# The seven-product input projection of an FFN, worked on two tiles at a time

## The chip, the cores and the metric

The kernel runs on one core of a Trainium2 chip. The metric is the device time of one execution in microseconds (us). The engines named here are TensorE (PE in the profile, with PEld for its weight loads), VectorE (DVE), ScalarE (ACT), GpSimd (POOL) and SyncE (SP), which issues the DMAs. SBUF is the on-chip memory of 128 partitions, PSUM the accumulators into which TensorE writes, in banks of 128 x 512 f32.

## The reference

Two layers of a decoder trunk on a residual stream h of 512 positions x 1024 channels, in f32. The FFN is computed four times, twice in each layer, with 2816 hidden columns:

```
def swiglu(h, w_in, w_out):
    gate, up = jnp.split(h @ w_in, 2, axis=-1)
    return (jax.nn.silu(gate) * up) @ w_out

h <- LN(alpha*h + 0.5*SwiGLU_a(h))            # FFN before mixing
h <- LN(alpha*h + W_o [GDN | SB | MLA](h))    # mixer
h <- LN(alpha*h + 0.5*SwiGLU_b(h))            # FFN after mixing
h <- h + sigmoid(h W_g) * (p[i] W_p)          # per-layer input embedding
```

The change concerns `h @ w_in`, the silu and the product of gate and up: the in-projection.

## The kernel before

An f32 operand is split into two fp32r parts, a high part `hi` (a cast) and a rest `lo = x - hi`, and each product is three matmuls, hi·hi, hi·lo and lo·hi, into one accumulator. The 2816 hidden columns are 22 tiles of 128. A tile has a gate and an up half, each 128 columns x 1024 rows of w_in, and a result of 128 x 512 for each half. In each FFN the first `NC` = 2 tiles are computed so. The other 20 go by a scheme of seven block products (Strassen in Winograd's form): the quarters of a tile's weights are a11, a12 (the gate half against the first and the second 512 channels) and a21, a22 (the same of the up half); sums of them, s1 to s4, and sums of quarters of the activations, t1 to t4, are multiplied, and the results are added up. A product is 4 steps of k x 3 matmuls of 256 columns, so a tile costs 7 x 12 = 84 matmuls, an in-projection 1680.

What a tile needs around them:

- Weights. `Weights` (lines 48 to 118) prepares blocks of 1024 columns, three blocks ahead of the one in use, in a pool of 4 hi and 4 lo buffers. For the seven products, `add_sums` (lines 78 to 107) puts two quarters of 512 in a block: four loads of a pair's tiles by eight DMAs of 256 KB, four sums of 512 columns a tile (line 96, VectorE), a cast for each of the seven items (line 97, ScalarE), and a subtraction for each (line 99): on VectorE for s1, s2 and s3, on GpSimd for a11, a12, a22 and s4.
- Accumulators. `open_tile` (line 510) takes one bank from each of two pools, psI for gate and psA for up. Each pool has two banks, so two tiles can be in flight; the banks of pools psB and psC are not used here.
- Evictions. `product` copies the results of b11, t1 and t2 to SBUF slabs on ScalarE (lines 503, 505 and 507). `close_tile` (lines 512 to 519) adds the gate half to a slab (514), applies silu on ScalarE, adds and copies the up half in three operations of 256 columns (516 to 518), and multiplies (519), on VectorE.

A tile framework schedules the program: it decides from a model of its own in which order each engine gets its instructions, and it adds the waits. The source order is therefore not the order on an engine; the order is fixed at build time, and each engine runs its list in order.

Behind the in-projection the out-projection multiplies the g tiles with w_out: `split_g` (lines 541 to 549) splits units of two g tiles into `gs` buffers, or, for four of the eleven units, into `old`, the buffers of the activations' hi and lo parts, which come free only after the last product that reads them. Its matmuls have 512 columns (`mm3`).

Of the kernel before, what the change touches and what calls it, by code (L numbers as in the profile page):

```python
# [17 lines left out]
P = 128  # L18
# [9 lines left out]
LAST = 4  # L28
OPT = [
# [18 lines left out]
class Weights:  # L48
# [29 lines left out]
    def add_sums(self, fs, sums, first=False):  # L78

        nc = self.nc  # L80
        rest = ("s1", "s4", "s2", "a22", "s3")
        if first:
            todo = [(0, "a11"), (0, "a12"), (1, "a11"), (1, "a12")] + [(f, n) for f in range(2) for n in rest]
        else:
            todo = [(f, n) for f in range(2) for n in ("a22", "a11", "a12", "s1", "s2", "s4", "s3")]
        quarters = [None, None]

        def one(f, name, hi, lo):
            if quarters[f] is None:
                r0, r1 = self.load(fs[f][0], sums("raw")), self.load(fs[f][1], sums("raw"))  # L90
                quarters[f] = {"a11": r0[:, 0:512], "a21": r0[:, 512:1024], "a12": r1[:, 0:512], "a22": r1[:, 512:1024]}
            q = quarters[f]
            if "s1" not in q and (name == "s1" or not first):
                for s, x, y, op in (("s1", "a21", "a22", ALU.add), ("s3", "a11", "a21", ALU.subtract), ("s2", "s1", "a11", ALU.subtract), ("s4", "a12", "s2", ALU.subtract)):
                    q[s] = sums(s)
# [3 lines left out]
            e.tensor_tensor(out=lo, in0=q[name], in1=hi.bitcast(F32), op=ALU.subtract)  # L99

        for i in range(7):
            def make(i=i):
                hi, lo = self.pair()
                for j in range(2):
                    one(*todo[2 * i + j], hi[:, j * 512:(j + 1) * 512], lo[:, j * 512:(j + 1) * 512])
                return hi, lo
            self.blocks.append(make)
# [12 lines left out]
def trunk(  # L120
# [128 lines left out]
    def new_xT():  # L249
        xT["hi"] = xp.tile([P, KD, S], F32R, tag="xh", name=nm("xh"))  # L250
        xT["lo"] = xp.tile([P, KD, S], F32R, tag="xl", name=nm("xl"))
# [76 lines left out]
    def plan_ffn(l, w_in, w_out):  # L328
# [4 lines left out]
        def sums(name):  # L333
            if ln_s["new"]:
                ln_s["new"] = False
                ln_s["n"] = 0
                u = unit("su").rearrange("p a b -> p (a b)")
                ln_s["r"] = 0
                ur = unit("wr").rearrange("p a b -> p (a b)")
                ln_s["w"] = [None, None, None, ur[:, 0:1024], ur[:, 1024:]]  # L340
                ln_s["s"] = [lnp.tile([P, 1024], F32, tag="lng", name=nm("sa")), lnp.tile([P, 1024], F32, tag="lnb", name=nm("sb")), u[:, 0:1024], u[:, 1024:]]
            if name == "raw":
                ln_s["r"] += 1
                return ln_s["w"][(ln_s["r"] - 1) % 5]
            i = ln_s["n"] = ln_s["n"] + 1
            i = (i - 1) % 8
            return ln_s["s"][i // 2][:, (i % 2) * 512:(i % 2 + 1) * 512]
# [4 lines left out]
        for f in range(NC, NF, 2):  # L352
            W.add_sums([tile_in(f), tile_in(f + 1)], sums, f == NC)
# [52 lines left out]

    ple_s = {}
# [12 lines left out]
    def ffn(l, ln_i):  # L420
# [3 lines left out]
        def part(ps, us, c0, c1):  # L424
            for j in range(2):
                for k in range(KD):
                    hi, lo = (u.rearrange("p (j k c) -> p j k c", k=4, j=2)[:, j, k % 4, :] for u in us[k // 4])
                    mm3(ps[j][:, c0:c1], hi, lo, xT["hi"][:, k, c0:c1], xT["lo"][:, k, c0:c1], k == 0, k == KD - 1)

        def g_(f):  # L430
            if f % 4 == 0:
                GA.append(unit("g"))
            return GA[f // 4][:, f % 4, :]

        def evac(f, ps):
            s = slab("s")
            act(s, ps[0], AF.Silu)
            V.tensor_tensor(out=g_(f), in0=s, in1=ps[1], op=ALU.mult)
# [3 lines left out]
        for f in range(2):  # L442
            part(pss[f], us[f], 0, 256)


        XH, XL = xT["hi"], xT["lo"]
        full = [unit("xf"), unit("xf")]

# [6 lines left out]
        R = {"b11": (XH[:, 0:4, 0:256], XL[:, 0:4, 0:256]), "b21": (XH[:, 4:8, 0:256], XL[:, 4:8, 0:256]), "b22": (XH[:, 4:8, 256:512], XL[:, 4:8, 256:512])}  # L455
        todo = []
        for name, x, y in (("t1", B[1, 2], B[1, 1]), ("t3", B[2, 2], B[1, 2]), ("t2", B[2, 2], "t1"), ("t4", B[2, 1], "t2")):
            if name == "t3":
                hl = [XH[:, 0:4, 256:512], XL[:, 0:4, 256:512]]
            else:  # L460
                hl = unit(name, F32R).rearrange("p a b -> p (a b)").rearrange("p (w k c) -> p w k c", w=2, k=4)
                hl = [hl[:, 0], hl[:, 1]]
# [6 lines left out]
        def split_t(name, hl, d):  # L469
            A.copy(hl[0], d)  # L470
            G.tensor_tensor(out=hl[1], in0=d, in1=hl[0].bitcast(F32), op=ALU.subtract)
# [5 lines left out]
        for f in range(2):  # L477
            part(pss[f], us[f], 256, 512)
            evac(f, pss[f])
        for f in range(2, NC):  # L480
            u = (W.next(), W.next())
            ps = banks(f % 2 == 1)
            part(ps, u, 0, 512)
            evac(f, ps)
        if NC > 2:
            split_t(*todo[1])
        blk = {"n": 0}

        def product(ps, name, start):
# [784 lines left out]
```

## Time and profile before

| | |
|---|---|
| median of 3 runs | 2470.91 us (2469.47 to 2471.38) |
| profiled execution | 2470.22 us |
| its span | 2468.4 us, 1.8 us less |
| TensorE busy | 2290.9 us, 93% of the span |
| VectorE busy | 1685.1 us, 68% |
| GpSimd busy | 1216.6 us, 49% |
| ScalarE busy | 1022.8 us, 41% |
| mean granted TensorE clock | 0.970 of full speed |

The four in-projections lie at 41.4 to 283.3, 814.3 to 1057.9, 1269.4 to 1507.9 and 2041.0 to 2284.7 us, from the first seven-product matmul to the last; these are 967.7 us of the span. The record of a matmul is longer than the distance to the next one, because matmuls overlap in the pipeline: the distance between two starts tells the rate. The same holds, less so, for the other engines.

### The profile page before, as it was taken

How to read it: one execution, taken by the hardware profiler on the slowest of the kernel's cores; microseconds unless marked ns; L12 is line 12 of the kernel's file. 1: busy time of each engine (PE TensorE's matmuls, PEld its weight loads, DVE VectorE, ACT ScalarE, POOL GpSimd, SP SyncE). 2: the span in 40 equal slices, each digit the busy share in tenths (PEclk: the TensorE clock that was granted, in tenths of full speed). 3: DMA queues.
4: the chain of work that ended last, by engine and by line, in shares of the span. 5: the costliest groups of instructions: out<-in, count | busy, mean ns of one | idle time of the engine just before them, and what ended most of it. 6: DMA issues, size and time to landing. Idle time of an engine off the chain costs nothing. (4 is left out here: it accounts for less than half of the span.)

```text
span 2468.4 us, 39369 instructions
## 1 busy us (share of the span) xinstructions
PE 2290.9 (93%) x15554; PEld 2000.7 (81%) x15554; DVE 1685.1 (68%) x2449; ACT 1022.8 (41%) x1929; POOL 1216.6 (49%) x785
## 2 busy tenths in 40 slices
PE   7999999998898899999989999999979997999998
PEld 7899888765777899988788998887657777999877
DVE  8899706559565899842589995075694668998334
ACT  4454513652452444532244544146424424445222
POOL 5555643434345655554365555424343466555542
PEclk9999999998999899999999999999999998999999
DMA  4333333211012233332323333332110122333322
GB/s 134 102 89 96 112 93 84 70 42 56 24 48 69 73 89 96 99 115 71 100 73 91 94 110 99 93 88 61 35 56 27 44 69 76 95 91 103 115 85 69
DMA packets 271272, 199.81 MB, mean 81 GB/s; under 512 B 12688, under 2 KB 236016, under 8 KB 271088
## 3 DMA queue, kind: packets, MB, share of 16 engines
q1 hardware_dynamic: 271088, 197.30, 27.2%
q8 instruction: 122, 2.00, 0.3%
q14 instruction: 62, 0.51, 0.1%
HBM read 195.17 MB, written 2.10 MB: 80 GB/s over the span
## 5 line engine op out<-in xcount | busy, mean ns | idle before, releaser
L74 POOL TENSOR_TENSOR wlo<-wraw,whi 128x1024 fp32r<-128x1024 f32 (+3 forms) x209 | 443.1, 2134 | 413.8 <-ACT whi L72 373.8
L72 ACT CAST whi<-wraw 128x1024 fp32r<-128x1024 f32 (+3 forms) x194 | 200.5, 1035 | 394.4 <-PE pi L405 156.7
L99 POOL TENSOR_TENSOR wlo<-wraw,whi 128x512 fp32r<-128x512 f32 x144 | 230.1, 1614 | 168.0 <-ACT whi L97 109.2
L499 PE MATMUL pa<-t,whi 128*128 128x256 f32 x640 | 191.3, 299 | 51.6 <-DVE g L518 27.9
L99 POOL TENSOR_TENSOR wlo<-wr,whi 128x512 fp32r<-128x512 f32 x96 | 153.9, 1616 | 132.7 <-ACT whi L97 127.9
L501 PE MATMUL pa<-t,wlo 128*128 128x256 f32 x640 | 177.8, 287 | 11.1 <-DVE wlo L99 11.1
L499 PE MATMUL pi<-xh,whi 128*128 128x256 f32 x640 | 185.5, 290 | 1.4 <-ACT whi L97 1.4
L501 PE MATMUL pa<-xh,wlo 128*128 128x256 f32 x640 | 182.1, 285 | 3.3 <-POOL wlo L99 3.3
L501 PE MATMUL pi<-xh,wlo 128*128 128x256 f32 x640 | 183.1, 286 | 0.0
L500 PE MATMUL pi<-xl,whi 128*128 128x256 f32 x640 | 183.0, 286 | 0.0
L500 PE MATMUL pa<-t,whi 128*128 128x256 f32 x640 | 182.9, 286 | 0.0
L499 PE MATMUL pa<-xh,whi 128*128 128x256 f32 x640 | 181.6, 284 | 0.0
L500 PE MATMUL pa<-xl,whi 128*128 128x256 f32 x640 | 181.6, 284 | 0.0
L499 PEld LDWEIGHTS pa<-t,whi 128*128 128x128 f32 x640 | 124.1, 194 | 67.2 <-DVE g L518 26.2
L187 ACT ACTIVATE s<-s 128x512 f32<-128x512 f32 x80 | 50.6, 632 | 258.2 <-DVE s L514 258.0
L97 ACT CAST whi<-su 128x512 fp32r<-128x512 f32 x160 | 91.7, 619 | 136.4 <-PE pi L500 118.9
L519 DVE TENSOR_TENSOR g<-g,s 128x512 f32<-128x512 f32 x80 | 140.2, 1752 | 1.1
L99 DVE TENSOR_TENSOR wlo<-su,whi 128x512 fp32r<-128x512 f32 x120 | 127.9, 1089 | 5.8 <-ACT whi L97 5.8
L501 PEld LDWEIGHTS pa<-t,wlo 128*128 128x128 f32 x640 | 121.9, 194 | 11.9 <-DVE wlo L99 11.9
L499 PEld LDWEIGHTS pi<-xh,whi 128*128 128x128 f32 x640 | 125.1, 195 | 3.8 <-ACT whi L97 1.9
L501 PEld LDWEIGHTS pa<-xh,wlo 128*128 128x128 f32 x640 | 123.5, 193 | 3.9 <-POOL wlo L99 3.9
L501 PEld LDWEIGHTS pi<-xh,wlo 128*128 128x128 f32 x640 | 124.9, 195 | 0.5 <-POOL wlo L99 0.4
(492 smaller groups left out, 7319.1 us busy)
## 6 DMA issues: line engine op xcount, KB each, us to landing
wraw<-in_ffa_w_in_dram SPq DMA_DIRECT2D x112, 256.0 KB, 3.8
wraw<-in_ffb_w_in_dram SPq DMA_DIRECT2D x112, 256.0 KB, 3.5
wraw<-in_ffa_w_out_dram SPq DMA_DIRECT2D x44, 512.0 KB, 3.8
wraw<-in_ffb_w_out_dram SPq DMA_DIRECT2D x44, 512.0 KB, 3.8
wraw<-in_mix_w_in_dram SPq DMA_DIRECT2D x40, 512.0 KB, 3.9
wr<-in_ffa_w_in_dram SPq DMA_DIRECT2D x64, 256.0 KB, 3.0
wr<-in_ffb_w_in_dram SPq DMA_DIRECT2D x64, 256.0 KB, 3.0
wraw<-in_mix_w_o_dram SPq DMA_DIRECT2D x16, 512.0 KB, 3.8
```

What stands on the lines that cost most here:

```text
L72: self.nc.scalar.copy(hi[:, :width], raw[:, :width])
L74: (eng or self.nc.gpsimd).tensor_tensor(out=lo[:, c], in0=raw[:, c], in1=hi[:, c].bitcast(F32), op=ALU.subtract)
L97: nc.scalar.copy(hi, q[name])
L99: e.tensor_tensor(out=lo, in0=q[name], in1=hi.bitcast(F32), op=ALU.subtract)
L187: i = A.activation(*a, **k)
L499: T.matmul(dst, ah, bh, start=start and k == 0, stop=False, skip_group_check=True)
L500: T.matmul(dst, ah, bl, start=False, stop=False, skip_group_check=True)
L501: T.matmul(dst, al, bh, start=False, stop=k == 3, skip_group_check=True)
L519: V.tensor_tensor(out=g, in0=g, in1=s, op=ALU.mult)
```

## The change

Two neighbouring tiles (a pair) are worked on together. `add_quads` replaces `add_sums`: a block is one quarter item of both tiles, 1024 columns wide. Per pair there are four DMAs of 512 KB instead of eight of 256 KB, four sums instead of eight, seven casts and seven subtractions instead of fourteen each. s3 and s4 are written over a21 and a12. Only the subtractions of a22 and a12 are GpSimd's (`LOG`), the other five are VectorE's. Seven raw slots of 1024 columns take the place of five.

Each product runs over both tiles before the next one starts. `open_pair` takes the four banks of psI and psA for every second pair, and the four of psB and psC for the others, so four tiles are in flight, and four slabs per pair out of the same pool of four. t3 also is copied out by ScalarE (line 496 of the changed kernel), into the slab that holds t1's copy; `close_pair` then needs one addition of 512 columns for the up half (507) in place of three operations of 256. The order of the products is t4 b11 b21 t1 t2 b22 t3, in the first pair b11 b21 t1 t2 t4 b22 t3. Besides, the activations' hi and lo buffers become one tile, and the out-projection takes its first four accumulators from psI and psA alone (`ps0`).

```
+LOG = ("a22", "a12")
-    def add_sums(self, fs, sums, first=False):
+    def add_quads(self, parts, slot, eng, first=False):
+        nc, q = self.nc, {}
+        def one(name):
+            if not q:
+                for n in ("a22", "a11", "a12", "a21"):
+                    q[n] = self.load([(lambda r: r.rearrange("p (k c) -> p k c", k=4), parts[n])], slot("raw"))
+                q["s3"], q["s4"] = q["a21"], q["a12"]
+            if "s1" not in q and name[0] == "s":
+                q["s1"], q["s2"] = slot("s1"), slot("s2")
+            for s, x, y, op in (("s1", "a21", "a22", ALU.add), ("s2", "s1", "a11", ALU.subtract), ("s4", "a12", "s2", ALU.subtract), ("s3", "a11", "a21", ALU.subtract)):
+                if s == name:
                     nc.vector.tensor_tensor(out=q[s], in0=q[x], in1=q[y], op=op)
+            hi, lo = self.pair()
             nc.scalar.copy(hi, q[name])
-            e = nc.vector if name in ("s1", "s2", "s3") else nc.gpsimd
+            eng(name).tensor_tensor(out=lo, in0=q[name], in1=hi.bitcast(F32), op=ALU.subtract)
+        def product(ps, name, w):
+            for f in range(2):
+                bank_ = ps["up" if up else "gate"][f]
...
+                elif name == "t3":
+                    A.copy(ps["x"][f][:, 0:256], dst)
-        def open_tile():
-            return {"gate": ibank(), "up": bank(), "s": slab("s"), "s5": slab("s5", 256)}
+        def open_pair(i):
+            b = banks4() if i % 2 == 0 else banks() + banks(True)
+            return {"gate": b[:2], "up": b[2:], "s": [slab("s"), slab("s")], "x": [slab("x"), slab("x")], "begun": set()}
-            V.tensor_tensor(out=g[:, 256:], in0=s5, in1=up[:, 256:], op=ALU.add)
-            V.tensor_copy(s5, up[:, 256:])
-            V.tensor_tensor(out=g[:, 0:256], in0=s5, in1=up[:, 0:256], op=ALU.add)
-            V.tensor_tensor(out=g, in0=g, in1=s, op=ALU.mult)
+        def close_pair(f0, ps):
+            g = g_(f0, 2)
+            for f in range(2):
+                V.tensor_tensor(out=ps["s"][f], in0=ps["s"][f], in1=ps["gate"][f], op=ALU.add)
+                act(ps["s"][f], ps["s"][f], AF.Silu)
+                V.tensor_tensor(out=g[:, f], in0=ps["x"][f], in1=ps["up"][f], op=ALU.add)
+            for f in range(2):
+                V.tensor_tensor(out=g[:, f], in0=g[:, f], in1=ps["s"][f], op=ALU.mult)
-        ps0 = banks() + [ibank(), ibank()]
+        ps0 = banks4()
```

VectorE in the middle of the first in-projection, before (s, s_44: slabs; su, sa, sb: sums; pi, pa: banks; wlo: a block's lo part):

```order
L514 TENSOR_TENSOR s_783<-s_783,pi_781 128x512
L99 TENSOR_TENSOR wlo_889<-su_273,whi_888 128x512
L516 TENSOR_TENSOR g_906<-s_44_784,pa_782 128x256
L96 TENSOR_TENSOR su_273<-wraw_1044 128x512
L96 TENSOR_TENSOR su_273<-wraw_1047,su_273 128x512
L517 COPY s_44_784<-pa_782 128x256
L518 TENSOR_TENSOR g_906<-s_44_784,pa_782 128x256
L99 TENSOR_TENSOR wlo_969<-sa_275,whi_968 128x512
L519 TENSOR_TENSOR g_906<-g_906,s_783 128x512
L96 TENSOR_TENSOR sa_275<-wraw_1185,wr_274 128x512
L99 TENSOR_TENSOR wlo_1001<-sb_276,whi_1000 128x512
```

The same stretch of VectorE in the changed kernel (x: the new slabs; wq, wraw: raw slots; s_70, s_80: the sums s1 and s2):

```order
L505 TENSOR_TENSOR s_983<-s_983,pi_979 128x512
L507 TENSOR_TENSOR g_969<-x_984,pa_980 128x512
L509 TENSOR_TENSOR g_969<-g_969,s_982 128x512
L92 TENSOR_TENSOR wq_270<-wq_270,s_70_1219 128x1024
L95 TENSOR_TENSOR wlo_1222<-s_69_1218,whi_1221 128x1024
L507 TENSOR_TENSOR g_969<-x_985,pa_981 128x512
L92 TENSOR_TENSOR s_80_1451<-wraw_1344,wq_270 128x1024
L95 TENSOR_TENSOR wlo_1251<-s_70_1219,whi_1250 128x1024
L509 TENSOR_TENSOR g_969<-g_969,s_983 128x512
L92 TENSOR_TENSOR wraw_1344<-wraw_1341,wraw_1344 128x1024
L95 TENSOR_TENSOR wlo_1282<-wq_270,whi_1281 128x1024
L92 TENSOR_TENSOR s_81_1452<-s_80_1451,wraw_1341 128x1024
```

A tile's chain of 512- and 256-column operations has become one of 512- and 1024-column operations for two tiles, with the next pair's sums and subtractions between them, and the subtractions of a11 and s4 now stand on VectorE.

ScalarE at the end of the first in-projection, before (gs and old: the split of g for the out-projection; nea: a preparation for the mixer):

```order
L505 COPY s_117_2954<-pi_2951 128x256
L546 CAST gs_3183<-g_906 128x1024
L546 CAST gs_3216<-g_1415 128x1024
L546 CAST gs_3379<-g_2435 128x1024
L72 CAST whi_3032<-wraw_3030 128x1024
L507 COPY s_2953<-pa_2952 128x256
L187 ACTIVATE s_2953<-s_2953 128x512
L195 ACT_TABLE_LOAD
L187 ACTIVATE nea_3933<-par_3902 128x8
L72 CAST whi_3080<-wraw_3078 128x1024
L546 CAST old_3250<-g_1925 128x1024
L546 CAST old_3249<-g_1415 128x1024
```

The same place in the changed kernel:

```order
L187 ACT_TABLE_LOAD
L179 ACTIVATE nea_3701<-par_3670 128x8
L496 COPY x_2609<-pc_2605 128x256
L73 CAST whi_2850<-wraw_2848 128x1024
L496 COPY x_2610<-pc_2606 128x256
L528 CAST old_3019<-g_1434 128x1024
L528 CAST old_3019<-g_1898 128x1024 x2
L528 CAST old_3019<-g_2362 128x1024
L528 CAST gs_2854<-g_462 128x1024
L528 CAST gs_2887<-g_462 128x1024
```

Before, six casts into gs stand ahead of the last tile's copies; now the copies of the last product and the four casts into old stand ahead of the first cast into gs. On TensorE all matmuls of the out-projection now stand behind the last product; before, some stood between the products of the last tiles. This holds for the first and the third in-projection; in the second and fourth the casts into gs stand first.

## Rows read from the trace of the kernel before

**Rows 1.** the page's first part: the span, and each engine's busy time.

```profile
span 2468.4 us, 39369 instructions
PE 2290.9 (93%) x15554; PEld 2000.7 (81%) x15554; DVE 1685.1 (68%) x2449; ACT 1022.8 (41%) x1929; POOL 1216.6 (49%) x785
```

**Rows 2.** windows of the four in-projections: length, busy us (x instructions) by engine, clock, DMA.

```profile
41.40:283.30 241.90, 221.89 (x1721) 214.63 (x1720) 214.02 (x239) 116.24 (x232) 136.77 (x84) 0.98 0.32 91
...
sum 967.70, PE 885.10 PEld 856.43 DVE 860.72 ACT 458.64 POOL 552.25; mean PE 221.27 PEld 214.11 DVE 215.18 ACT 114.66 POOL 138.06
```

**Rows 3.** windows of 180 us in the middle of each in-projection, same columns.

```profile
80.00:260.00 180.00, 167.86 (x1352) 163.61 (x1353) 163.78 (x195) 86.05 (x181) 102.37 (x66) 1.00 0.35 100
...
sum 720.00, PE 675.67 PEld 659.20 DVE 659.48 ACT 343.13 POOL 405.27; mean PE 168.92 PEld 164.80 DVE 164.87 ACT 85.78 POOL 101.32
```

**Rows 4.** timeline, TensorE, steady: start, duration, engine, line, operation, tiles.

```profile
152.06 0.28 PE L499 MATMUL pa<-xh,whi 128*128 128x256 f32 x1
152.18 0.28 PE L500 MATMUL pa<-xl,whi 128*128 128x256 f32 x1
...
272.66 0.39 PE L403 MATMUL pb<-whi,gs 128*128 128x512 f32 x1
272.89 0.39 PE L404 MATMUL pb<-wlo,gs 128*128 128x512 f32 x1
```

**Rows 5.** waits of TensorE in 80 to 260 us: total, times, longest.

```profile
PE pa L499 <- DVE g L518: 6.4, 9, 1.2
PE pa L499 <- ACT s L503: 5.3, 6, 1.0
```

**Rows 6.** windows of the first microseconds of two in-projections, columns as in rows 2.

```profile
41.40:60.00 18.60, 12.65 (x80) 12.04 (x78) 18.44 (x14) 8.44 (x17) 15.54 (x8) 0.82 0.16 43
814.30:835.00 20.70, 11.77 (x78) 10.87 (x77) 20.67 (x15) 8.38 (x15) 17.75 (x9) 0.76 0.13 38
```

**Rows 7.** waits of TensorE in 814.3 to 855 us, as rows 5.

```profile
PE pa L501 <- DVE wlo L99: 5.1, 1, 5.1
PE pi L501 <- DVE wlo L99: 3.9, 2, 3.3
```

**Rows 8.** timeline, VectorE, before the second in-projection, little on GpSimd beside it.

```profile
800.26 0.68 DVE L96 TENSOR_TENSOR sa<-wraw,wraw 128x512 f32<-128x512 f32 x1
800.86 0.68 DVE L96 TENSOR_TENSOR sa<-wraw 128x512 f32<-128x512 f32 x1
...
806.42 1.22 DVE L453 TENSOR_TENSOR xf<-xh,xl 128x1024 f32<-128x1024 f32 x1
807.55 2.32 DVE L465 TENSOR_TENSOR xf<-xf,xf 128x1024 f32<-128x1024 f32 x1
```

**Rows 9.** operations on the FFN tiles: engine, operation, tiles, count, duration min/median/max ns, starts, shape.

```profile
L518 DVE TENSOR_TENSOR g<-s,pa x80: 407/420/422, 70.6 to 2285.9; 128x256 f32<-128x256 f32 x80
L519 DVE TENSOR_TENSOR g<-g,s x80: 679/1779/2583, 72.7 to 2286.4; 128x512 f32<-128x512 f32 x80
L547 DVE TENSOR_TENSOR gs<-g,gs x28: 1210/1214/3428, 270.1 to 2297.9; 128x1024 fp32r<-128x1024 f32 x28
L547 DVE TENSOR_TENSOR old<-g,old x16: 1212/2311/3434, 287.5 to 2294.5; 128x1024 fp32r<-128x1024 f32 x16
```

**Rows 10.** GpSimd by line and shape: busy us, mean ns, idle before.

```profile
L74 POOL TENSOR_TENSOR wlo<-wraw,whi 128x1024 fp32r<-128x1024 f32 x139 | 353.7, 2552 | 318.1 <-ACT whi L72 285.2 <-issue 26.0 <-DVE gs L547 6.8
L99 POOL TENSOR_TENSOR wlo<-wraw,whi 128x512 fp32r<-128x512 f32 x144 | 230.1, 1614 | 168.0 <-ACT whi L97 109.2 <-PE pi L501 53.2 <-PE pa L501 4.2
```

**Rows 11.** timeline, ScalarE, end of the first in-projection.

```profile
267.08 2.94 ACT L546 CAST gs<-g 128x1024 fp32r<-128x1024 f32 x3
...
280.68 1.28 ACT L195 ACT_TABLE_LOAD   x1
...
284.38 3.89 ACT L546 CAST old<-g 128x1024 fp32r<-128x1024 f32 x4
```

**Rows 12.** page, DMA issues: count, KB each, us from issue to landing.

```profile
wraw<-in_ffa_w_in_dram SPq DMA_DIRECT2D x112, 256.0 KB, 3.8
```

More of the change, by code (lines that the diff above doesn't have):

```diff
@@ L76, in add @@
         self.blocks.append(make)
-    def add_sums(self, fs, sums, first=False):
[L80 to L95, printed above, removed]
+    def add_quads(self, parts, slot, eng, first=False):
[9 more added lines that the diff above has]
+                if s == name:
@@ L109, in fill @@
+            return hi, lo
+        for name in ("a11", "a12", "s1", "s2", "a22", "s4", "s3") if first else ("a22", "a11", "a12", "s1", "s2", "s4", "s3"):
+            self.blocks.append(lambda name=name: one(name))
     def fill(self, n):
@@ L331, in tile_in, with slot, quarter_rows @@
                       rows(w_in, l, kh * 4, 4, j * D_FF + f * P, j * D_FF + (f + 1) * P)) for j in range(2)] for kh in range(2)]
-        def sums(name):
+        def slot(name):
             if ln_s["new"]:
[L335 to L347, printed above, removed]
+                ln_s["new"], ln_s["r"] = False, 0
+                ln_s["w"] = [x[:, i * 1024:(i + 1) * 1024] for x in (unit("wq").rearrange("p a b -> p (a b)") for _ in range(2)) for i in range(2)]
+            if name != "raw":
+                return lnp.tile([P, 1024], F32, tag="lng" if name == "s1" else "lnb", name=nm(name))
+            ln_s["r"] += 1
+            i = (ln_s["r"] - 1) % 7
+            return ln_s["w"][i // 2] if i % 2 == 0 else None
+        def quarter_rows(f, i, j):
+            return rows(w_in, l, j * 4, 4, i * D_FF + f * P, i * D_FF + (f + 2) * P)
         for f in range(NC):
@@ L352, in plan_ffn @@
         for f in range(NC, NF, 2):
-            W.add_sums([tile_in(f), tile_in(f + 1)], sums, f == NC)
+            W.add_quads({f"a{i + 1}{j + 1}": quarter_rows(f, i, j) for i in range(2) for j in range(2)}, slot,
+                        lambda name: G if name in LOG else V, f == NC)
         for n in range(2):
@@ L422, in ffn, with part @@
         GA = []
[L424 removed]
+        X = xT["x"]
+        XH, XL = xT["hi"], xT["lo"]
+        def part(ps, us, c0):
             for j in range(2):
@@ L477, in ffn @@
         for f in range(2):
[L478 removed]
+            part(pss[f], us[f], 256)
             evac(f, pss[f])
[L480 to L489, printed above, removed]
[L490 to L507 removed]
@@ L539, in ffn @@
+        for i, f in enumerate(range(NC, NF, 2)):
+            ps = open_pair(i)
+            for name in ("b11", "b21", "t1", "t2", "t4", "b22", "t3") if i == 0 else ("t4", "b11", "b21", "t1", "t2", "b22", "t3"):
+                product(ps, name, W.next())
+                if i == 0 and name == "b21":
+                    split_t(*todo[1])
+            close_pair(f, ps)
         NU = NF // 2
@@ L556, in split_unit @@
             if not spare:
-                old = [xp.tile([P, KD, S], F32R, tag=tag, name=nm("old")) for tag in ("xh", "xl")]
-                spare.extend(o[:, 4 * i:4 * i + 4, :] for o in old for i in range(2))
+                old = xp.tile([P, 2, KD, S], F32R, tag="x", name=nm("old"))
+                spare.extend(old[:, j, 4 * i:4 * i + 4, :] for j in range(2) for i in range(2))
             return spare[len(HL) - 5]
```

84 lines of the change are left out of this document (27 added, 57 removed).

## The prediction

> **What bounds the kernel now.** I read the page's engine totals first, then windows over the four in-projections and over their middles, then TensorE's waits in these, then single durations on VectorE and GpSimd, and last ScalarE at an in-projection's end. The reader should see in the totals that TensorE is busy 93% of the span [rows 1], which alone would say that there is little to win. The windows say more. The four in-projections take 967.7 us [rows 2]. Steady seven-product matmuls start 0.12 us apart (152.06, 152.18), those of 512 columns 0.23 us apart [rows 4]. An in-projection window holds 1680 of the first kind and about 41 of the second (1721 in all), which at these distances need 201.6 + 9.4 = 211.0 us; four need 844. So about 124 us are lost in the four windows, to waits and to a low clock, and this is what the change can win. The change leaves the number of matmuls as it is.
>
> Where the loss lies: in the middles, 720 us hold 5443 matmuls (1352 in the first window) [rows 3], worth 653 us; 67 us are lost there, 2.06 us in each pair of 168 matmuls (22.2 us where 20.16 would do). TensorE waits there only for L499, the first product of a tile into a bank, and for the operations that empty that bank: L518 of VectorE, 9 times, and the copy L503 of ScalarE, 6 times [rows 5]. Two tiles hold all banks, so each tile's start waits for an earlier tile's emptying. VectorE is busy 659 of these 720 us, 91.6%: it comes late because it is nearly full, and it is full because its operations stretch. A 512-column operation from SBUF follows the next one 0.60 us later when alone (800.26, 800.86), a 1024-column one after 1.13 [rows 8]; the multiplication L519 of the same 512 columns takes 1779 ns at the median, 679 at the least, while L518, which reads PSUM, stays between 407 and 422 ns [rows 9]. GpSimd's 405 us of the 720 [rows 3] are what stands beside the stretched ones. The rest, 124 - 67 = 57 us, is at starts and ends. The first window of 18.6 us holds 80 matmuls (9.6 us), the second of 20.7 us 78 (9.4 us), at granted clocks of 0.82 and 0.76 [rows 6]; the longest waits there are for lo parts that VectorE makes (5.1 and 3.3 us) [rows 7].
>
> **The change part by part.** *Evictions and sums on VectorE.* Per pair, before: 14 SBUF operations of 512 for sums and lo parts, two additions (L514) and two multiplications of 512, six operations of 256. Alone: 18 x 0.6 + 6 x 0.45 = 13.5 us. Measured, 91.6% of 22.2 = 20.35 us, so 6.85 us of stretch for 56% x 22.2 = 12.5 us of GpSimd, 0.55 us for each. After: four sums and five lo parts of 1024, 9 x 1.13 = 10.2; two multiplications, two additions L505 and two L507 of 512, 6 x 0.6 = 3.6; together 13.8 us alone. The own work hardly changes; what changes is GpSimd's, from eight halves to two lo parts of 1024 per pair, at 2.55 us each [rows 10] 5.1 us. At 0.55 this gives a stretch of 2.8 us and 16.6 us for VectorE, against the 20.16 that TensorE needs. The bounds: no stretch, 13.8; each of the nine wide operations at the 2.31 us of the split into old, the multiplications at 1.78 [rows 9], 9 x 2.31 + 2 x 1.78 + 4 x 0.6 = 26.8 us, which would pass TensorE. I take 16.6, since in this count two operations of GpSimd can only meet a few of VectorE's.
>
> At the multiplication L519, alone 679 ns and with GpSimd busy 1779, against the steady 407 to 422 of L518, the trace shows that only operations with both inputs in SBUF stretch [rows 9]. The Trainium skill ("SBUF — State Buffer", section Who interferes with whom) says that such an operation and a GpSimd operation that reads SBUF exclude one another, for the whole instruction. The trace agrees in kind. By that rule two blocks of 2.55 us would add at most 5.1 us a pair, an estimate, and VectorE would need 18.9 us; that speaks for the change even in its harder form.
>
> *ScalarE.* Seven casts of 1024 (2.94 us for three [rows 11], 0.98 each) 6.9 us, eight copies of 256 at some 0.36 and two silus: about 11 of 20.16 us. It was busy 343 of 720 us [rows 3], 10.6 a pair. Its load costs nothing; its order may, below.
>
> *Banks.* Four tiles in flight instead of two. The pair that starts finds the banks of the pair before last, emptied about 16 us ago by the walk below. The waits of rows 5 go. What comes next is a wait for a lo part, the blocks being three ahead. I walked the new orders with the durations above, beginning at the end of a pair's last product: VectorE has emptied that pair's banks 7 us later; the lo parts of s1, s2, s4 and s3 are ready at 3.4, 6.3, 9.1 and 11.4 us and wanted at 8.6, 11.5, 14.4 and 17.3. Margins of 5 to 6 us, more than the 2.8 (and the 5.1) of stretch. A pair is then bound by TensorE. I count 0.2 us a pair of small losses, 36 pairs, 7 us; before, the same pairs lost 2.06 each, 74.
>
> *DMAs.* The same 2 MB a pair, in four issues of 512 KB instead of eight of 256 KB; each of the old took 3.8 us to land [rows 12]. Seven raw slots let the loads of a pair go out before the one ahead is done. They land before they are wanted by the walk, and cost nothing; if this cover goes, s1 is late by some 1 to 5 us a pair.
>
> *Starts.* The first pair still makes nine wide lo parts and sums on VectorE with no blocks ahead of it. Before, the two windows of rows 6 lost 9.0 and 11.3 us (length less matmuls by 0.12). After, with order b11 b21 t1 t2, the lo part of s2 is the late one, by my walk 2 us in the second in-projection, with a granted clock that falls after the wait; I take 2 + 5 + 1.5 + 1.5 = 10 us for the four first pairs and 3 for the plain tiles ahead of them.
>
> *Ends.* Here the change makes it worse. In the first and third in-projection ScalarE makes the copies of t3, a cast, and then four casts into old (3.89 us [rows 11]) before it casts the first gs for the out-projection. In before six gs casts stood ahead (267.08, beside the last tiles), and matmuls of the out-projection filled TensorE's waits. After, all of them stand behind the last product; the last copy ends 1.9 us after it, the four old casts 5.8, gs 6.9, and its lo part, queued behind four of VectorE, about 9. Only the matmuls that need no lo part can start before. I count 7 us idle plus some 2.5 at a lower clock: from rows 6, 0.82 over 18.6 us is 6.7 us at half speed, each of which costs half. So 9.5 us each at two ends; at the other two, where gs goes first, 1.5 each. Together 22 us. Bounds: 1.5 at each end (6), and 14 at the bad ones (31).
>
> *The rest.* The merged hi and lo tile and the mixer's order, moved in some dozens of places by an instruction or two, I cost at nothing, between -4 and +6 us; 1526 us of the span do not belong to the in-projections.
>
> The sum: 124 us lost before; after 7 + 10 + 3 + 22 = 42. The gain is 82 us, on the profiled execution of 2470.2 us (2468.4 + 1.8): 2388. The median lies 0.7 higher: 2389. Since the walk takes every operation at its ordinary duration I add 2 us: **2391 us**, 3.2% faster. The likeliest case's own range is 2375 to 2410.
>
> **The rivals.**
> *A. A queue ties the pairs together.* All four slabs of the pool belong to one pair. ScalarE copies b11 of the next pair into one of them, which has to wait until VectorE's multiplication of the pair before (L509) has read it; behind the copy wait the casts of the next blocks, and behind these TensorE. For it: ScalarE works strictly in order, and is idle in half of its time, waiting for others; VectorE's lead over it is two or three operations. Against it: the walk has L509 done 1 us ahead of b11's copy when two additions come promptly. If each pair loses 1 us, 36 us come back: 2427; it lies between 2410 and 2445. The same number would come from loads that are late.
> *B. Better than the walk.* The ends cost 1.5 us each and the starts half: 16 + 7 us back, 2366 to 2374. For it: the scheduler's order could hide the old casts behind matmuls that wait for no lo part.
> *C. Nothing to win.* VectorE still needs 21 to 22 us a pair, since a 1024-column operation waits longer for GpSimd, and only starts gain: 2450 to 2470. For it, 807.55 with 2.32 us for a wide one [rows 8].
> *D. Slower.* VectorE becomes the bound. Each of its nine wide operations meets GpSimd and takes 2.31 us; 26.8 us a pair from the bound above, 4.6 more than now, over 36 pairs +166, less some 20 of better starts: about 2615. It decides from the point where VectorE's work on a pair passes 22.2 us. For it: the split into old shows 2311 ns as its median [rows 9], and VectorE has taken over a11's and s4's subtraction. Against it: those splits stand right behind an in-projection, where GpSimd works on the lo parts of w_out one after the other (2.55 us each [rows 10]), while here it is busy 5.1 of 20 us.
>
> **How the numbers follow.** The forecast's case 58%, A 20%, B 13%, C 4%, D 5%. The range from 2366 (B) to 2440 (all but the upper end of A) leaves out D, C and little else. A measurement of this kernel can tell 0.2%, 4.9 us, from no change: the forecast, A and B and the greater part of C are faster, 0.92; 0.02 for the same; D and what I may have overlooked 0.06.
>
> **What would show it.** In the changed profile the middles should have some 1480 to 1500 matmuls in 180 us instead of 1352, with no waits of TensorE on evictions; VectorE at 16 to 17.5 us a pair, 80 to 87%, and GpSimd near 25%; a gap of about 7 us on TensorE behind the last product of the first and third in-projection, on casts and lo parts of gs, and none of that size at the other two. Waits for ScalarE's casts, spread over all pairs, would show A; wide operations of VectorE at over 2 us throughout D. I am wrong if the middles stay at 22 us a pair.

## The result, and the profile after

The changed kernel takes 2403.74 us (median of 4 runs, 2402.83 to 2404.15) against 2471.14: a ratio of 0.972, 95% interval 0.970 to 0.974. The forecast was 2391, between 2366 and 2440. The profiled execution's span is 2402.4 us, 66.0 less than before. The page's first lines, where the span is and which engines lost work:

```profile
span 2402.4 us, 38041 instructions
PE 2278.9 (95%) x15554; PEld 2002.6 (83%) x15554; DVE 1449.0 (60%) x2089; ACT 1033.4 (43%) x1729; POOL 913.5 (38%) x545
```

Against [rows 1] VectorE lost 236 us of busy time and GpSimd 303, TensorE 12. Where the 66 us come from is seen when the span is cut at the same places in both kernels: first seven-product matmul, last matmul of the out-projection, and so on. One of these places needs care. In the changed kernel's fourth FFN two seven-product matmuls start at 1996.82 us, ahead of 44 matmuls of the two plain tiles, which take 5.28 us; everywhere else in the two kernels the plain tiles come first. The cut there is therefore put at 2002.10, so that each window holds the same work as the kernel before's (2231 matmuls from there on in both). Windows of the changed kernel (length, then busy us by engine with the instructions, granted clock, DMA share, GB/s):

```profile
40.25:378.70 338.45, 327.31 (x2219) 304.79 (x2218) 184.25 (x193) 148.32 (x213) 117.81 (x50) 0.98 0.32 96
378.70:814.96 436.26, 399.76 (x2851) 318.42 (x2849) 280.00 (x570) 187.10 (x395) 171.96 (x153) 0.92 0.20 56
814.96:1143.80 328.84, 326.58 (x2231) 304.39 (x2230) 196.21 (x197) 148.86 (x216) 126.71 (x50) 0.99 0.32 98
1143.80:1244.54 100.74, 89.44 (x486) 77.13 (x484) 62.16 (x63) 32.83 (x44) 46.13 (x21) 0.92 0.32 99
1244.54:1577.00 332.46, 325.26 (x2220) 303.09 (x2219) 181.79 (x191) 145.94 (x210) 113.98 (x48) 0.99 0.31 93
1577.00:2002.10 425.10, 393.64 (x2850) 312.74 (x2849) 279.95 (x568) 187.20 (x394) 175.19 (x154) 0.94 0.20 58
2002.10:2332.30 330.20, 326.00 (x2231) 304.18 (x2230) 196.50 (x199) 149.04 (x216) 119.20 (x48) 0.99 0.31 97
2332.30:2402.40 70.10, 59.61 (x261) 48.18 (x259) 34.92 (x43) 16.86 (x23) 23.33 (x11) 0.94 0.25 83
```

The same cuts of the kernel before:

```profile
41.40:395.30 353.90, 333.89 (x2220) 307.38 (x2219) 248.24 (x281) 145.84 (x263) 191.30 (x108) 0.99 0.31 91
395.30:814.30 419.00, 385.68 (x2851) 306.11 (x2849) 274.22 (x569) 186.63 (x396) 178.23 (x155) 0.96 0.20 57
814.30:1171.20 356.90, 335.20 (x2231) 308.90 (x2230) 254.28 (x288) 146.95 (x264) 193.26 (x108) 0.98 0.31 92
1171.20:1269.40 98.20, 88.80 (x485) 76.39 (x484) 63.90 (x65) 32.90 (x47) 48.17 (x21) 0.95 0.29 86
1269.40:1619.90 350.50, 332.61 (x2220) 305.50 (x2220) 246.24 (x279) 143.08 (x257) 190.24 (x108) 0.99 0.32 93
1619.90:2041.00 421.10, 387.83 (x2849) 308.67 (x2848) 274.37 (x570) 188.12 (x398) 177.18 (x156) 0.96 0.20 57
2041.00:2398.10 357.10, 334.09 (x2231) 307.90 (x2230) 254.40 (x287) 145.22 (x263) 193.92 (x107) 0.98 0.31 92
2398.10:2468.40 70.30, 59.53 (x261) 48.02 (x259) 34.93 (x43) 16.81 (x23) 23.26 (x11) 0.94 0.24 83
```

The four FFNs (first, third, fifth, seventh row) fall from 1418.4 to 1330.0 us, 88.4 less. The rest of the program gives back a quarter of that. The first layer's mixer (second row) rises from 419.0 to 436.3 us, at a granted clock of 0.92 instead of 0.96, and the second layer's (sixth row) from 421.1 to 425.1, at 0.94 instead of 0.96. The stretch between the layers (fourth row) takes 2.5 us more. The start before the first row is 1.2 us shorter, the last row 0.2. That is 88.4 + 1.2 + 0.2 - 17.3 - 4.0 - 2.5 = 66.0.

The middles of the in-projections after (the first of four windows, and their sum), to lay beside [rows 3]:

```profile
80.00:240.00 160.00, 160.00 (x1336) 160.00 (x1335) 113.28 (x118) 85.58 (x135) 39.09 (x16) 1.00 0.35 106
...
sum 560.00, PE 560.00 PEld 560.00 DVE 396.05 ACT 301.57 POOL 135.90; mean PE 140.00 PEld 140.00 DVE 99.01 ACT 75.39 POOL 33.98
```

160 us hold 1336 matmuls, 0.120 us each: the pace of [rows 4], without a loss. VectorE is busy 70.7%, 14.3 us of a pair's 20.16, and GpSimd 24%.

TensorE's waits in the whole changed kernel (total, times, longest); these three lines are the longest of those in the seven products and the out-projections:

```profile
PE pi L394 <- ACT gs L528: 12.8, 2, 6.4
...
PE pa L402 <- DVE wlo L95: 5.3, 3, 4.0
...
PE pi L402 <- DVE wlo L95: 3.6, 1, 3.6
```

The waits for evictions of [rows 5] are gone from the middles; a single one of 1.0 us, for a copy of t1, is left at the start of the second in-projection. What else is left are lo parts at the starts and the two waits of 6.4 us at the ends.

### The profile page after: what moved, and what is told of

The parts are those of the page before. It is cut to its first block, busy times and chain, and to the rows that moved or that the text cites. A ratio compares the mean times of both kernels' runs of the same rounds, so it can differ in the third digit from the quotient of the medians.

```text
span 2402.4 us, 38041 instructions
## 1 busy us (share of the span) xinstructions
PE 2278.9 (95%) x15554; PEld 2002.6 (83%) x15554; DVE 1449.0 (60%) x2089; ACT 1033.4 (43%) x1729; POOL 913.5 (38%) x545
## 4 chain that ended last, share of the span: by engine, by line
PE 81%; DVE 13%; issue 3%; ACT 1%; POOL 1%; DMA 0%; SPq 0%; POOLq 0%; ACTq 0%; DVEq 0%
PE pi L394 5%; PE pi L396 5%; PE pi L395 5%; PE pc L402 4%; PE pc L401 4%; PE pc L400 4%; PE pa L402 3%; PE pa L401 3%; PE pa L400 3%; PE pb L401 3%; PE pb L402 3%; PE pb L400 3%; PE pc L394 2%; PE pc L396 2%; PE pc L395 2%
## 5 line engine op out<-in xcount | busy, mean ns | idle before, releaser
L73 ACT CAST whi<-wraw 128x1024 fp32r<-128x1024 f32 (+3 forms) x194 | 200.7, 1036 | 421.1 <-PE pa L396 189.1
L95 POOL TENSOR_TENSOR wlo<-wq,whi 128x1024 fp32r<-128x1024 f32 x48 | 124.8, 2601 | 288.9 <-ACT whi L94 270.3
L94 ACT CAST whi<-wq 128x1024 fp32r<-128x1024 f32 x116 | 121.7, 1049 | 129.3 <-issue 34.9
L95 DVE TENSOR_TENSOR wlo<-wq,whi 128x1024 fp32r<-128x1024 f32 x68 | 89.1, 1312 | 74.7 <-ACT whi L94 74.7
L400 PE MATMUL pb<-x,whi 128*128 128x256 f32 x448 | 129.2, 292 | 4.6 <-ACT x L246 4.6
L401 PE MATMUL pb<-x,whi 128*128 128x256 f32 x448 | 130.5, 292 | 0.0
L402 PE MATMUL pb<-x,wlo 128*128 128x256 f32 x448 | 129.4, 290 | 0.0
L400 PE MATMUL pc<-x,whi 128*128 128x256 f32 x448 | 127.0, 285 | 0.6 <-DVE h L291 0.6
L401 PE MATMUL pc<-x,whi 128*128 128x256 f32 x448 | 126.7, 283 | 0.0
L402 PE MATMUL pc<-x,wlo 128*128 128x256 f32 x448 | 126.4, 283 | 0.0
L95 DVE TENSOR_TENSOR wlo<-s,whi 128x1024 fp32r<-128x1024 f32 x80 | 109.0, 1363 | 2.0 <-ACT whi L94 2.0
L394 PE MATMUL pi<-x,whi 128*128 128x512 f32 x256 | 101.9, 398 | 1.4 <-DVE gc L699 1.4
L396 PE MATMUL pi<-x,wlo 128*128 128x512 f32 x256 | 101.9, 398 | 0.0
L395 PE MATMUL pi<-x,whi 128*128 128x512 f32 x256 | 101.7, 397 | 0.0
```

Source lines behind the costliest of these rows:

```text
L73: self.nc.scalar.copy(hi[:, :width], raw[:, :width])
L95: eng(name).tensor_tensor(out=lo, in0=q[name], in1=hi.bitcast(F32), op=ALU.subtract)
L394: T.matmul(ps, ah, bh, start=first, stop=False)
L395: T.matmul(ps, ah, bl, start=False, stop=False)
L396: T.matmul(ps, al, bh, start=False, stop=last)
L400: T.matmul(dst, ah, bhl[:, 0], start=first, stop=False, skip_group_check=True)
```

## The experiments

In the mixers' column of what follows, the length is from the last out-projection matmul's start to the first seven-product matmul. In three kernels (the changed one, one set of banks, none on GpSimd) 44 matmuls of the plain tiles come behind that matmul in the second layer; their 5.3 us are counted with the mixer here, and not with the FFN. So counted, the changed kernel's mixers take 436.6 and 425.5 us and its FFNs, from first to last matmul start, 1328.5. A long stretch is one of 24 us or more at half clock in the trace's clock records (the changed kernel: 687 to 718 and 1882 to 1909 us). Where no range is given, the time is that of a single execution; the kernel before took 2465 to 2479 us on the same chips.

**One set of banks.**

```
-            b = banks4() if i % 2 == 0 else banks() + banks(True)
+            b = banks4()
```

> The changed kernel with one part undone: every pair takes the same four banks (psI, psA), none alternates; pairs, wide sums, evictions and GpSimd's share stay. My account: in the changed kernel TensorE runs without a wait in the middles because the next pair finds banks that were emptied long before. With one set the first product of a pair (t4, into the up banks) waits until VectorE's additions L507 have read them, about 1.1 us after the last product for the first tile and 2 to 3 for the second: 1.5 to 3 us a pair, 36 pairs, 2455 to 2510 us. Rival: the gain came from VectorE's lighter load (fewer and wider operations, less of GpSimd beside them), and banks cost little: 2404, at most 2420 us.

2415.7 us (2411.95 to 2424.82; ratio to before 0.978, 0.976 to 0.981). The four FFNs together take 1337.3 us, 8.8 more than in the changed kernel, and the middles keep the full pace. My estimate of 1.5 to 3 us a pair was wrong. The first window of the middles:

```profile
80.00:240.00 160.00, 160.00 (x1336) 160.00 (x1335) 113.86 (x117) 85.15 (x135) 38.54 (x16) 1.00 0.34 102
```

In the trace the scheduler has changed the order at a pair's start: t4 and b11 of the first tile, then b21, which goes into the gate banks, and only then the second tile's t4 (from 115.04 us on, where the first tile's began at 108.92). That leaves VectorE's additions time. The alternating banks are not what the gain in the middles rests on, once the order may adapt.

**GpSimd's share, up and down.**

```
-LOG = ("a22", "a12")
+LOG = ("a22", "a12", "a11", "s4")      (and, in a second kernel, LOG = ())
```

> The changed kernel with GpSimd making the lo parts of four items (a22, a12, a11, s4) as before, VectorE those of three. My account: VectorE's own work falls to 11.5 us a pair, GpSimd's rises from 5.1 to about 10.4, and at 0.55 us of stretch for each the sum is 17.2, still under TensorE's 20.16: the in-projections stay as they are, 2404 us, with some us of either sign from the second layer's mixer, whose order changes a little. Rival: GpSimd's share is what slowed VectorE in the kernel before; with it back, VectorE stretches beyond 20.16 us a pair: 2430 us and more.

> The changed kernel with no lo part of the seven products on GpSimd; VectorE makes all seven. VectorE's work alone is 16.0 us a pair, with next to no stretch. My account: TensorE remains the bound, 2404 us. The order of TensorE's instructions in both mixers is that of the changed kernel, so the two long stretches at half clock (30.7 us in the first layer's mixer from 687 us on, 27.3 us in the second's) should show again. Rival: VectorE near its limit, late in each pair: 2430 us and more. Second rival, on the clock: the stretches are chance and go, 2390 us.

With four on GpSimd: 2438.2 us, 34 above what I expected. That is the rival's number, but not its mechanism: VectorE stays at 72% (405.64 of 560 us in the middles). The FFNs take 22.6 us more; the waits there are single ones for lo parts (3.5 and 4.0 us at the longest), nearly all near the starts. The second mixer takes 13.1 more, its long stretch at half clock lasting 38 us instead of 27. With none on GpSimd: 2402.1 us, as forecast, with the two long stretches (31 and 24 us) where the changed kernel has them. TensorE's order in both mixers is there the changed kernel's, matmul by matmul.

**The order at the ends.** An order edge, no wait of its own:

```
+                if u < 2:
+                    CS.append((i, j))
+                elif 5 <= u <= 8:
+                    for x, y in CS:
+                        tc.add_manual_dep(i.ins, x.ins.name, NOSYNC, reason="gs first")
+                        tc.add_manual_dep(j.ins, y.ins.name, NOSYNC, reason="gs first")
```

> The changed kernel with an order edge added: ScalarE's casts and VectorE's lo parts into old may not come before those of the first two gs. My account of the ends: in the first and third in-projection the wait of 6.4 us for the cast of gs and the low clock behind it (6.8 us at half) go: -16 to -18 us. The mixers' order on TensorE moves as a side effect, near to that of the kernel before. If the mixer's order is what brings the half clock there, the layer 0 mixer falls back by some 15 us too: 2370 to 2376 us; if the half clock has another cause and stays, 2386 to 2390. Rival: the old casts came first because the gs buffers are not free earlier, and nothing moves: 2400 to 2408.

2370.0 us (2368.21 to 2371.79), ratio to before 0.960, 0.957 to 0.962: better than both kernels. ScalarE and TensorE at the end of the first in-projection in the changed kernel, then with gs first:

```profile
250.11 3.89 ACT L528 CAST old<-g 128x1024 fp32r<-128x1024 f32 x4
253.90 2.94 ACT L528 CAST gs<-g 128x1024 fp32r<-128x1024 f32 x3
...
255.00 0.80 PE L394 MATMUL pi<-whi,gs 128*128 128x512 f32 x1 [6.38 <-ACT gs L528]
255.60 0.63 PE L395 MATMUL pi<-wlo,gs 128*128 128x512 f32 x1
```

```profile
249.92 4.84 ACT L528 CAST gs<-g 128x1024 fp32r<-128x1024 f32 x5
...
251.03 0.50 PE L394 MATMUL pi<-whi,gs 128*128 128x512 f32 x1 [2.60 <-ACT gs L528]
```

The four casts of old, 3.8 us, stood in front; behind the longer wait the matmuls follow each other at half clock (0.80 and 0.63 us long, where [rows 4] have 0.39). The total lies in the expected range, but by other terms than I had named. The FFNs fall by 11.6 us, not by 16 to 18: a wait of 2.60 us for gs stays, and from the last product to the last matmul of the out-projection the first and the third FFN take 125.5 and 124.9 us instead of 130.0 and 129.7 (the other two 122.6). The first mixer falls from 436.6 to 417.3 us with its long stretch gone, as the expectation had it, and the second from 425.5 to 420.2, its stretch gone too. That the mixers moved at all is a side effect: an edge at the FFN's end changed the scheduler's order there.

**Parts of the change alone, on the kernel before.** Alternating banks:

```
+            n[0] += 1
+            return {"gate": ibank() if n[0] % 4 in (1, 2) else one(), "up": bank() if n[0] % 4 in (1, 2) else one(True), ...
```

> The kernel before with one thing of the change: every second two tiles take their banks from psB and psC, so four tiles can hold banks; single tiles, halves, evictions and GpSimd's share stay, and so do four slabs, two a tile. The order in both mixers is that of the kernel before, so the mixers should keep their times. If the banks were what bound it, VectorE's 20.35 us a pair becomes the bound and a pair falls from 22.2 to 20.4: 2405 us. My account after the run with one bank set: the banks alone are not it; the wait moves from the bank to the slab, since the copy of b11 needs a slab that the tile two before still holds until VectorE's last multiplication: 2445 to 2471 us.

a11 and s4 from GpSimd to VectorE:

```
-            e = nc.vector if name in ("s1", "s2", "s3") else nc.gpsimd
+            e = nc.gpsimd if name in ("a22", "a12") else nc.vector
```

> The kernel before with only the lo parts of a11 and s4 moved from GpSimd to VectorE. VectorE's work alone becomes 15.9 us a pair, GpSimd's falls from 12.5 to some 6.4, stretch by 0.55 to 3.5: 19.4 instead of 20.35 us. My account: TensorE's waits for banks stay, since each tile still waits for a VectorE that is 87% busy; up to 0.9 us a pair comes back, 32 us: 2440 to 2465 us, and the second layer's mixer, whose order becomes that of the changed kernel, can lose some 10 us to a low clock. Rival: GpSimd's share alone was the brake: 2400 to 2415 us.

The new evictions:

```
+            elif name == "t3":
+                A.copy(ps["s5"][:, 0:256], dst)
-            V.tensor_tensor(out=g[:, 256:], in0=s5, in1=up[:, 256:], op=ALU.add)
-            V.tensor_copy(s5, up[:, 256:])
-            V.tensor_tensor(out=g[:, 0:256], in0=s5, in1=up[:, 0:256], op=ALU.add)
+            V.tensor_tensor(out=g, in0=s5, in1=up, op=ALU.add)
```

> The kernel before with the new evictions alone: t3 copied out by ScalarE, one addition of 512 columns for the up half in place of three operations of 256; single tiles, one bank each. VectorE saves 1.5 us a pair (20.35 to 18.9 us) and the bank of the up half is free after one operation instead of three, some 0.8 us earlier. My account, after the run of pairs alone: the order by pairs carries most: 2440 to 2460 us, with waits for banks still there. Rival: the evictions carry it, and the middles reach TensorE's pace: 2400 to 2415 us.

2448.5, 2467.4 and 2477.4 us: at most a third of the gain, no gain, no gain. The first time lies in its expected range, the other two above theirs. The window 80 to 240 us of the kernel before, then of these three in turn:

```profile
80.00:240.00 160.00, 148.53 (x1193) 144.49 (x1194) 146.29 (x174) 75.98 (x160) 89.87 (x58) 1.00 0.34 95
```

```profile
80.00:240.00 160.00, 152.44 (x1227) 148.35 (x1226) 147.96 (x178) 76.33 (x161) 91.04 (x60) 1.00 0.35 99
```

```profile
80.00:240.00 160.00, 146.26 (x1152) 143.16 (x1151) 132.54 (x194) 73.74 (x153) 42.76 (x28) 0.97 0.33 92
```

```profile
80.00:240.00 160.00, 150.56 (x1218) 148.12 (x1216) 135.38 (x142) 77.98 (x170) 87.40 (x56) 0.99 0.33 95
```

1193 matmuls before, then 1227, 1152 and 1218, where 1336 would fit. The third window is the telling one: with GpSimd's time more than halved VectorE is busy 83% instead of 91%, and TensorE loses more, in the other three middles too. (At the starts this kernel is better: its FFNs together take 5.3 us less than before, and its second mixer, with a long stretch, 4.7 more.) So it was not VectorE's load as such. VectorE's timeline in that kernel, and TensorE's matmul that waited, show what else:

```profile
104.37 0.69 DVE L96 TENSOR_TENSOR su<-wr,wraw 128x512 f32<-128x512 f32 x1 [2.34 <-DMA wraw<-in_ffa_w_in_dram]
...
105.70 0.68 DVE L514 TENSOR_TENSOR s<-s,pi 128x512 f32<-128x512 f32 x1
...
112.03 0.41 DVE L518 TENSOR_TENSOR g<-s,pa 128x256 f32<-128x256 f32 x1
...
112.50 0.58 PE L499 MATMUL pa<-t,whi 128*128 128x256 f32 x1 [2.10 <-DVE g L518]
```

A sum (L96) waits 2.34 us for its load, and the eviction L514 stands behind it in the queue; L518, which frees the bank, comes at 112.03, and TensorE's matmul at 112.50 waited 2.10 us for it. In this window VectorE waits 11.6 us for loads, in the kernel before 5.2; in the middles of the changed kernel and of the next one it waits for none.

**Pairs alone.** The changed kernel with one set of banks, four lo parts on GpSimd, and every sum, cast and lo part in two halves (the two edits above, and):

```
+                    for h in H:
+                        nc.vector.tensor_tensor(out=q[s][:, h], in0=q[x][:, h], in1=q[y][:, h], op=op)
+            for h in H:
+                nc.scalar.copy(hi[:, h], q[name][:, h])
+                eng(name).tensor_tensor(out=lo[:, h], in0=q[name][:, h], in1=hi[:, h].bitcast(F32), op=ALU.subtract)
```

> The changed kernel with all else undone: one set of banks, GpSimd making four lo parts, and each sum, cast and lo part in two halves of 512. What stays: products over two tiles, the new evictions, sums made when they are wanted, in place. If the order by pairs carries the gain: VectorE 12 us alone and 5.7 to 6.9 of stretch, under 20.16; middles stay near TensorE's pace, 2435 to 2455 us with the mixers' low clocks of the run with four lo parts on GpSimd. Rival: each part carries a share, so that without them the pairs fall back to some 22 us: 2470 us and more.

and pairs with the evictions of before (the opposite of the edit above):

> The changed kernel with the evictions of before: no copy of t3, three operations of 256 columns on PSUM for each tile's up half. VectorE gets 1.5 us more a pair, about 15.5 of 20.16. My account: the middles stay at TensorE's pace, 1336 matmuls in 160 us; 2395 to 2412 us, the mixers' order being another one. Rival: the short chain behind t3 is what frees the banks in time: waits for banks of 1 us and more a pair, 2440 us and more.

2425.2 and 2382.5 us, both below their expected ranges. Pairs alone, the same window and the sum of the four middles:

```profile
80.00:240.00 160.00, 160.00 (x1336) 160.00 (x1335) 126.07 (x157) 90.19 (x191) 92.16 (x65) 1.00 0.32 100
...
sum 560.00, PE 560.00 PEld 560.00 DVE 439.79 ACT 319.03 POOL 325.36; mean PE 140.00 PEld 140.00 DVE 109.95 ACT 79.76 POOL 81.34
```

The full pace, with GpSimd as busy as before (58%) and halves of 512. So the gain in the middles needs neither wide operations, nor more banks, nor less of GpSimd. Outside the middles these are worth something together: the FFNs take 1352.9 us here, 24.4 more than in the changed kernel, 24.0 of them between the first and the last seven-product matmul. The old evictions do no harm, and were 21 us faster than the new: with them the scheduler puts gs first at the ends (FFNs 1308.4 us, 20.1 less than in the changed kernel; 122.0 us from the last product to the last matmul in all four); the second mixer took 437.0 us, with a long stretch of 31.

**No lo part on GpSimd, gs first.**

> The kernel with gs first, and all seven lo parts on VectorE. The two gains are apart from each other: 2370 less the 5 us that the in-projections gained without GpSimd: 2363 to 2368 us, with the mixers' order and clock as with gs first. Rival: VectorE, at 16 us a pair, comes late behind the ends and starts: 2370 to 2380 us.

2378.9 us (2374.97 to 2382.05), ratio 0.963, 0.961 to 0.966: no gain on 2370.0, as the rival had it. The FFNs took 2.1 us more, the rest of the span 6.

**TensorE kept busy in the mixer.** In each step of the recurrence:

```
                 if c < 7:
                     ps = bank()
+                    for _ in range(8):
+                        T.matmul(ps[:, 256:512], xT["hi"][:, 0, 0:P], xT["hi"][:, 0, 0:256], start=True, stop=True)
```

> The changed kernel with eight matmuls of 256 columns more in each of seven steps of the mixer's recurrence (GDN scan) in either layer; their results are not used. They are 56 x 0.12 = 6.7 us of TensorE's work a layer at full clock, in a stretch in which TensorE waits for other engines. If the 17 us that the first layer's mixer lost come from TensorE's half clock from 687 to 718 us, and the clock fell because TensorE had too little to do there: the half-clock stretches of 30.7 and 27.3 us shrink or go, the first mixer falls from 436.6 us to 422 to 430, the second from 420 to 412 to 420; 2385 to 2400 us in all. Rival: the time lies in the changed order itself (a longer chain of waits), the low clock being only its mark: the mixers become longer by the added work, 2405 to 2418 us.

The same in the kernel with pairs and old evictions:

> Pairs with the evictions of before (2382.5 us, with a half-clock stretch of 31 us in the second layer's mixer, which took 437.0 us) and the unused matmuls in the mixer's recurrence. If the low clock there costs the 15 to 17 us that the mixers with such a stretch show: the stretch goes, the second mixer falls to some 420 us, the first stays at 421 or gains a little: 2360 to 2370 us. Rival: the added 6.7 us a layer eat it, or the order changes for the worse: 2378 to 2390 us.

2393.6 us, and 2374.8 (2371.52 to 2377.53; ratio 0.960, 0.958 to 0.963). The windows of the changed kernel around the long stretch, those of the kernel before at the same work, and the filled kernel's:

```profile
660.00:687.00 27.00, 25.84 (x276) 21.84 (x277) 12.12 (x38) 9.93 (x27) 5.77 (x7) 1.00 0.09 24
687.00:718.00 31.00, 30.48 (x211) 23.93 (x208) 13.70 (x40) 11.11 (x26) 10.73 (x9) 0.50 0.09 32
```

```profile
676.00:703.00 27.00, 27.00 (x292) 23.43 (x291) 11.06 (x40) 10.39 (x28) 4.45 (x6) 1.00 0.11 33
703.00:734.00 31.00, 26.80 (x255) 21.19 (x254) 24.58 (x64) 17.61 (x39) 22.51 (x18) 0.89 0.17 52
```

```profile
687.00:718.00 31.00, 28.26 (x301) 22.84 (x300) 22.13 (x54) 19.70 (x43) 22.62 (x18) 0.94 0.16 52
378.70:804.50 425.80, 391.74 (x2906) 314.51 (x2905) 277.51 (x570) 187.07 (x395) 172.72 (x153) 0.95 0.20 58
```

In the changed kernel the clock is 0.50, the level of 1.2 GHz, for 31 us, after 27 us with 276 matmuls at full clock; TensorE is busy 30.48 of the 31 us, VectorE 13.70. The kernel before had 292 matmuls in as long a time, and its clock fell for 6.8 us only. With the added matmuls the stretch is gone and the first mixer takes 426.2 us instead of 436.6, though it does more. The second mixer, whose stretch of 27 us went too, stayed at 425.8 after 425.5, not as I expected. In the other filled kernel the second mixer fell from 437.0 to 427.9, the first, which had no stretch, rose from 421.1 to 425.7. If the added work costs these 5 us in every mixer, a stretch of 31 us costs about 10 + 5 = 15, and that of 27 us about 5; both are estimates. The second kernel's time missed its range, because I left out the 5 us a mixer. The runs do not part the low clock from the order: with the added matmuls the scheduler also placed others anew. Of the first mixer's 2850 matmuls and transposes 126 start more than 20 places from where they stood in the changed kernel (from the kernel before to the changed one it was 199). All mixers of the kernels without filling, sorted:

| half-clock stretch in the mixer | mixers | length, us |
|---|---|---|
| none of 24 us | 13 | 417.3 to 423.6 |
| 24 to 27 us | 4 | 425.2 to 427.3 |
| 31 to 38 us | 7 | 435.0 to 438.9 |

Why 4 us more at half clock go with some 10 us more of length is not explained by these runs.

## Why the prediction was right, and where its sum was off

1. *The middles.* The forecast had 7 us lost in 36 pairs where before lost 74; measured, nothing is lost. VectorE was put at 16.6 us a pair and takes 14.3. The mis-sized term is the stretch: 0.5 us where 2.8 was taken. Between 80 and 240 us VectorE's lo parts of 1024 take 1211 ns, what [rows 8] show for such an operation alone (1.22 us), while the multiplication of 512 still stretches to 829:

```profile
L95 DVE TENSOR_TENSOR wlo<-s,whi 128x1024 fp32r<-128x1024 f32 x16 | 19.4, 1211 | 0.0
...
L509 DVE TENSOR_TENSOR g<-g,s 128x512 f32<-128x512 f32 x16 | 13.3, 829 | 0.3
```

The rule of the Trainium skill ("SBUF — State Buffer", section Who interferes with whom) that the prediction used as the harder form allows 5.1 us a pair by the estimate made there; the trace, with 0.5, stays far below it. That only operations with both inputs in SBUF stretch, as the prediction put it, is more than [rows 9] show: they show that L519 stretches and L518 does not.

2. *Why TensorE waited.* I had said that VectorE came late because it was nearly full, and counted the freed banks as the cure. The runs speak against both as a full account: less load alone gained nothing, banks alone 22 us, and pairs gain with one set of banks. What the trace of the kernel with less GpSimd shows is VectorE waiting for a load, with evictions queued behind. That this wait is also what held the kernel before was not shown. Which property of the pairs cures it was not taken apart: the order of the products, sums made only when they are wanted, seven raw slots and the four larger loads are in all the kernels with pairs. It stays open.

3. *Starts and ends.* The bad ends were forecast at 9.5 us each, 8 more than the good ones. From the last product to the last matmul of the out-projection the first and third FFN take 130.0 and 129.7 us, the second and fourth 122.6: 7.4 and 7.1 more, with the wait of 6.4 us that the prediction had described. The starts were taken too low: from the first to the last product the in-projections take 208.1, 205.8, 202.4 and 207.2 us, where 1680 matmuls need 201.6; as the middles lose nothing, that is 17 us at the four starts instead of 10. All of the FFNs were to gain 82 us, and gained 88.4. That it is so close is partly luck, since the single terms were off by some us in both directions.

4. *The rest.* This step failed: "The merged hi and lo tile and the mixer's order ... I cost at nothing, between -4 and +6 us". It cost 17.3 us in the first mixer, 4.0 in the second and 2.5 between the layers. The order of TensorE's instructions changed by more than an instruction or two: of the first mixer's 2850, 818 start more than two places from where they stood, and 199 more than 20. The matmuls came thinner (276 in 27 us instead of 292), and the clock stayed at half for 31 us. The step's bounds were taken from the length of the moves, not from what a thinner stretch does to the clock, though [rows 6] had shown a clock of 0.76 after such waits. How much of the 17.3 us is the clock's and how much the order's own stays open, as said above. Together the 24 us are more than the 12.7 between forecast and result; the FFNs gave some back. The time fell into the range because the range was wide enough for this miss, not because the step was foreseen. (By [rows 2] 1500.7 us of the span lie outside the in-projections, not 1526; the sum does not use this number.)

5. *The rivals.* No wait for a slab (A) shows; the ends (B) could be had, but only in another kernel, with an order edge or with the old evictions; VectorE did not become the bound (C, D): in the middles its wide operations took 1.21 us, not 2.31.

## What to carry to other kernels

When a scheduler orders the program, compare its order far from the edit too: here a part that was hardly edited took back a quarter of the gain. Judge an engine that stands in the way by what waits in its queue in front of the late instruction, not by its busy share. Before two windows are compared, count the instructions in them: 44 matmuls on the other side of a cut are worth 5 us here, more than the second mixer lost. And take each part of a change out alone: GpSimd's smaller share gained nothing on the kernel before and was worth 34 us beside the pairs, most of it at the starts and in a mixer, the second set of banks was worth 12, and undoing the new evictions made the kernel 21 us faster.

## What had not been expected of the hardware

Half clock lasted 31 to 38 us in seven mixers of the kernels run here, and each such mixer took 435 to 439 us against 417 to 424 without. Unused matmuls, 6.7 us of work a layer, removed the stretch, though the order changed with them, and made the first mixer of the changed kernel 10.4 us shorter. With stretches of 24 to 27 us, in the second layer's mixer, it took 425 to 427.
